# Order of the mLSTM gate rows, state loads and last normalisations around an RWKV-7 / mLSTM scan

## The chip, the cores and the metric

The kernel runs on one core of one Trainium2 chip. A core has five engines that run side by side, each through its own list of instructions: PE (matmul; its weight loads are shown apart as PEld), DVE (vector), ACT (scalar), POOL (GpSimd) and SP (here it only issues DMAs). An engine takes its instructions strictly in order, and an instruction that waits for a semaphore holds all behind it. DMAs are issued by SP, ACT or POOL, each into its own queue. The metric is the device time of one execution in microseconds; of the kernel before, three runs gave 2306.32, 2308.16 and 2311.97 us, so a median of 2308.16.

## The reference

One layer of a diffusion trunk, on 128 context tokens and 1024 latent tokens of width 1024. The context reads only itself; the latent tokens start each scan from a given state.

```python
h = rmsnorm(x, norm_g[0]) * (1 + sc1) + sh1           # sc1, sh1, g1 ... from silu(cond) @ ada_w
z_r, z_m, z_g = split(h @ w_in)                       # RWKV, mLSTM, branch gates
y_r, S = rwkv7_bidir(centred_shift(z_r), S0, ...)     # 8 heads x 64, both directions
y_m, (C, n, m) = mlstm_bidir(z_m, C0, n0, m0, ...)    # 4 heads x 128, both directions
merged = sigmoid(gr) * (y_r @ w_branch_rwkv) + sigmoid(gm) * (y_m @ w_branch_mlstm)
x = x + g1 * rmsnorm(merged @ w_out)
... gated ConvFFN: up, depthwise conv, silu, product, down
```

RWKV-7 updates a 64x64 state for each head, token and direction: `S = S*w - (S@kk) (kk*a)^T + v k^T`, `y = S@r`. The two directions are added, and each head is normalised over its 64 values (mean and variance), scaled, increased by a bonus term and multiplied by a gate `sigmoid(gd) @ g_up`. The mLSTM keeps a 128x128 state `C`, a vector `n` and a running maximum `m` for each head and direction. Its weights are exponentials of sums of gate logarithms less that maximum; its output, both directions added, is normalised over 128 values and gated by `sigmoid(o)`. The final states of the context are outputs.

## The kernel before

Tokens lie in nine blocks of 128, block 0 the context. Four parts follow one another, with overlap.

**Projection and preparation** (up to about 640 us): the combined projection in two-term products (`whi` and `wlo` times `act`, results in `pg`, copied out as `zraw` by ACT), the operands of both scans, and the triangular systems of all RWKV chunks (`La`, `Lb`, lines 522 and 524, on DVE and POOL).

**RWKV scan**: 18 steps over chunks of 64 tokens, both directions at once. `ORDER` gives the two chunks of a step: two context steps, then sixteen latent ones. `back` of step n begins with the matmuls `pP` (the state times the chunk's keys), which ACT copies to `Pm` (line 891). It goes on through `pU`, `pN` (the new state, `sn`) and `pY` (the outputs, copied or added into `ysum`). Between these stand, by `between(n)`, the `front` matmuls of step n+1 (`psc`, `pbk`, `pmh`, `pmt`, `pmb`; their results are copied by ACT as `A`, `BT`, `HT`, `TT` and masked by DVE as `KA`, `AB`), and groups of 24 projection matmuls by `fill` (the matmuls `pg` of the branch gates). `suv` holds a step's states and values; its values are loaded on POOL's queue (line 791), `XN` too (832); `KA`, `BKs` and the `TT` pieces are loaded on SP. Step 1's result is the context's final state; the latent steps start from `st`, loaded between (steps 1 and 2).

`rpost(b)` normalises a finished block b: a first half (mean, sum of squares, scaling of `ysum`) and a second half (transposes `pgt`, then scale, bonus `bon`, gate `pgg`, and the store `yrd`). `POST` tells after which step a block is begun: `{1: 0, 11: 4, 12: 5, 13: 3, 14: 6, 15: 2, 16: 7}`; blocks 1 and 8 follow after the last step. The two halves are apart by most of a step.

**mLSTM**: nine chunks of 128 for each direction, in 18 calls of `mback`, `mfront` one or two ahead. Its gate rows (`gates()`, six pieces) turn the gate logarithms of all tokens into tables, through sums, a running maximum along the chunks (`mm`, `mpv`) and a round trip through memory that turns it from rows into columns (`mpd` out, `mc` in, lines 1037 to 1044). `mback` ends with the outputs `hsum`, `mfinish` normalises a chunk.

**Merge, output projection, ConvFFN**: from about 1200 us; `y2r` and `y2m` are made from `yrd` and `ymd`, which come back from memory.

**What sets the order.** A scheduler lays out each engine's list by times that it simulates, from the program order and the dependences; so what has no late operand moves up. Instructions marked `keep_in_program_order` stay among each other as written. Before, this holds only for PE's, by an `Ordered` wrapper that is switched on from the scan to the end of the mLSTM. The gate pieces are written after steps 3 to 8, yet their rows are free to move. Tiles of a pool with one name, or tag, share memory: the next tile waits until the last one is read.

Of the kernel before, what the change touches and what calls it, by code (L numbers as in the profile page):

```python
# [57 lines left out]
def _body(tc, ctx, A, O, dbg, stop):  # L58
    nc = tc.nc
    v, s, gp = nc.vector, nc.scalar, nc.gpsimd  # L60
    dma = nc.sync.dma_start
# [13 lines left out]

    class Ordered:

        on = False

        def matmul(self, *a, **k):  # L80
            return self.keep(nc.tensor.matmul(*a, **k))  # L81

        def transpose(self, *a, **k):
            return self.keep(nc.tensor.transpose(*a, **k))
# [843 lines left out]
    def finish_ctx(sn):  # L928
        for d in range(2):
            pt = pss([128, 4, 64], "pfs")  # L930
            for p, h, hr in HP:
                pe.matmul(pt[hr, p, :], sn[hr, d, p, :], ident[hr, hr], start=True, stop=True)
            so = cp.tile([128, 4, 64], F32, name="so", tag="sn2", bufs=1)
            v.tensor_copy(so, pt)
            dma(O["s_rwkv"][0, 0, d].rearrange("(p h) i j -> (h i) p j", h=2), so)
# [657 lines left out]
```

## Time and profile before

| what | value |
|---|---|
| median of three runs | 2308.16 us (2306.32 to 2311.97) |
| the profiled execution | 2310.34 us, its span 2308.6 us |
| mean granted PE clock | 0.959 |
| PE busy | 2109.4 us, 91% |
| DVE busy | 1361.5 us, 59% |
| ACT busy | 847.8 us, 37% |
| POOL busy | 572.8 us, 25% |
| first `pP` of the scan | 650.49 us |
| last `pP` of the scan | 966.52 us |
| first latent `pmN` of the mLSTM | 1057.91 us |

All positions are microseconds from the span's start. A row of the timeline gives start, duration, engine, line, operation, `out<-in` and, in brackets, how long the engine stood idle before it and what released it. A row of a window gives its length, the busy time of PE, PEld, DVE, ACT and POOL with their instruction counts, the granted PE clock, the busy share of the DMA engines and GB/s. A row of a tile gives min/median/max in nanoseconds and the first and last start. A row of a group gives its count, then busy time and mean nanoseconds, then the idle time before, with what ended it. An engine's name with a q is its sequencer, which issues DMAs. Ordered calls carry the line of the wrapper (L81, L84), not of their own.

### The profile page before, as it was taken

The numbers are of one execution on the slowest core, as the hardware profiler recorded it, in microseconds if no ns is written. First come the engines' busy times: TensorE is split into PE (matmuls) and PEld (weight loads), VectorE is DVE, ScalarE is ACT, GpSimd is POOL, SyncE is SP. The second block draws the span as 40 slices with busy tenths as digits, with TensorE's granted clock in tenths as the row PEclk, the third lists the DMA queues.
The fourth block names the chain that finished last, engine by engine and source line by source line (L and its number), as shares of the span: only waits on it lengthen the run. The fifth ranks groups of instructions, "written<-read, shape, count | busy, mean of one in ns | idle before, by whom it ended". The sixth has DMA issues, their size and how long they took to land. (4 is left out here: it accounts for less than half of the span.)

```text
span 2308.6 us, 39893 instructions
## 1 busy us (share of the span) xinstructions
PE 2109.4 (91%) x16323; PEld 1944.2 (84%) x16323; DVE 1361.5 (59%) x2140; ACT 847.8 (37%) x1746; POOL 572.8 (25%) x725
## 2 busy tenths in 40 slices
PE   6999998988868998868869999999999999999996
PEld 4998998977857887868768978999999999999995
DVE  3666779789344556423544365646565656565558
ACT  3663646462233444445532143432212222222213
POOL 2000289888422233234612212000000000000004
PEclk9999998999978998979979999999999999999999
DMA  9144444445654554456657642202111111111104
GB/s 259 52 102 113 126 125 115 129 118 135 166 97 120 140 148 112 114 152 199 207 186 221 199 151 96 64 29 64 56 46 45 48 55 46 46 46 55 41 24 164
DMA packets 391413, 254.55 MB, mean 110 GB/s; under 512 B 86305, under 2 KB 368069, under 8 KB 391232
## 3 DMA queue, kind: packets, MB, share of 16 engines
q1 hardware_dynamic: 246864, 144.88, 22.6%
q10 hardware_dynamic: 135840, 88.03, 13.1%
q0 software_dynamic: 8528, 19.10, 3.3%
q8 instruction: 128, 2.10, 0.4%
q14 instruction: 53, 0.43, 0.1%
HBM read 186.73 MB, written 65.23 MB: 109 GB/s over the span
## 5 line engine op out<-in xcount | busy, mean ns | idle before, releaser
L81 PE MATMUL pg<-act,whi 128*128 128x384 f32 (+1 forms) x4416 | 856.0, 341 | 8.6 <-ACT zraw L537 5.6
L81 PEld LDWEIGHTS pg<-act,whi 128*128 128x128 f32 (+1 forms) x4416 | 778.1, 190 | 24.4 <-ACT zraw L537 6.0
L81 PE MATMUL pg<-act,wlo 128*128 128x384 f32 (+1 forms) x2208 | 436.1, 337 | 7.7 <-DVE wlo L364 7.7
L81 PEld LDWEIGHTS pg<-act,wlo 128*128 128x128 f32 (+1 forms) x2208 | 388.0, 188 | 11.2 <-DVE wlo L364 8.0
L364 DVE TENSOR_TENSOR wlo<-wraw,whi 128x1024 fp32r<-128x1024 f32 x130 | 163.5, 1259 | 217.8 <-ACT whi L363 217.6
L47 DVE SCALAR_TENSOR_TENSOR ua<-uraw,par,ua 128x945 f32<-128x945 f32 (+2 forms) x176 | 214.7, 1220 | 41.4 <-ACT ua L1485 38.2
L81 PE MATMUL pfd<-whi,f 128*128 128x512 f32 x792 | 227.5, 395 | 6.5 <-DVE facc L1557 6.5
L1559 POOL TENSOR_TENSOR x<-facc,grow 128x512 f32<-128x512 f32 x17 | 24.3, 1454 | 822.7 <-DVE facc L1557 822.7
L363 ACT ACTIVATE whi<-wraw 128x1024 fp32r<-128x1024 f32 x130 | 136.6, 1053 | 162.9 <-PE pg L81 103.3
L81 PEld LDWEIGHTS pfd<-whi,f 128*128 128x128 f32 x792 | 146.4, 188 | 37.2 <-DVE facc L1557 9.1
L1557 DVE TENSOR_TENSOR facc<-pfd,facc 128x512 f32<-128x512 f32 x180 | 122.1, 687 | 52.2 <-PE pfd L81 52.2
L524 POOL TENSOR_TENSOR Lb<-Lb,tmp 96x31 f32<-96x31 f32 (+15 forms) x155 | 130.3, 841 | 12.1
L522 POOL TENSOR_TENSOR tmp<-La,Lb 96x31 f32<-96x31 f32 (+15 forms) x155 | 121.2, 782 | 27.5 <-DMA La<-Ad 15.7
L81 PE MATMUL pfd<-wlo,f 128*128 128x512 f32 x396 | 122.6, 391 | 0.0
L1489 ACT ACTIVATE ua<-ua 128x1152 f32<-128x1152 f32 x22 | 25.7, 1168 | 219.4 <-DVE ua L47 219.4
L1499 ACT ACTIVATE f<-ua 128x384 fp32r<-128x384 f32 x66 | 32.1, 518 | 194.1 <-DVE ua L1498 194.1
L851 DVE TENSOR_TENSOR KA<-psc,msk 64x512 f32<-64x512 f32 x72 | 49.2, 684 | 84.2 <-ACT A L850 83.8
L81 PE MATMUL pwo<-whi,act 128*128 128x512 f32 x288 | 90.2, 393 | 1.1 <-ACT whi L363 1.1
L47 DVE SCALAR_TENSOR_TENSOR qacc<-zraw,par,qacc 128x945 f32<-128x945 f32 (+2 forms) x64 | 84.2, 1315 | 9.2 <-ACT qacc L580 8.7
L81 PEld LDWEIGHTS pfd<-wlo,f 128*128 128x128 f32 x396 | 74.3, 188 | 16.8
L791 POOL DMA_DIRECT2D suv<-Vd x72 | 42.5, 600 | 134.6 <-DVE sn L909 73.9
L1498 DVE TENSOR_TENSOR ua<-pg,ua 128x384 f32<-128x384 f32 x66 | 34.5, 553 | 68.9 <-PE pg L81 53.4
(368 smaller groups left out, 3085.0 us busy)
## 6 DMA issues: line engine op xcount, KB each, us to landing
wraw<-in_w_in ACTq DMA_DIRECT2D x44, 512.0 KB
wraw<-in_ffn_up ACTq DMA_DIRECT2D x44, 512.0 KB
zraw<-in_ada_w SPq DMA_DIRECT2D x24, 512.0 KB
wraw<-in_ffn_down ACTq DMA_DIRECT2D x22, 512.0 KB
KRd<-KR SPq DMA_DIRECT2D x24, 384.0 KB
sgz<-zraw ACTq DMA_DIRECT2D x16, 576.0 KB
KA<-KRd SPq DMA_DIRECT2D x72, 128.0 KB
BKs<-BKd SPq DMA_DIRECT2D x36, 256.0 KB
```

The costliest lines, as they stand in the source:

```text
L47: v.scalar_tensor_tensor(o, img[:, r0 + i:r1 + i, c0 + j:c1 + j], wt, o, op0=ALU.mult, op1=ALU.add)
L81: return self.keep(nc.tensor.matmul(*a, **k))
L363: s.activation(hi, raw, AF.Copy)
L364: v.tensor_tensor(lo, raw, hi.bitcast(F32), op=ALU.subtract)
L522: e.tensor_tensor(t3, L[:, j, i].unsqueeze(2).to_broadcast([NI, n, m]), X[:, j:j + 1, c].to_broadcast([NI, n, m]), op=ALU.mult)
L524: e.tensor_tensor(X[:, i, c], X[:, i, c], t3, op=ALU.subtract)
L791: pdma(suv[r, d, h].rearrange("t x p n -> t x (p n)"), src.unsqueeze(1).to_broadcast([64, 2, 4 * LC]))
L851: v.tensor_tensor(q.KA[orr, :, h, :], sc_[h][orr], msk[orr, d:d + 1, :].to_broadcast([64, 4, 128]), op=ALU.mult)
L1489: s.activation(ua, ua, AF.Silu)
L1498: v.tensor_tensor(ua[:, gs], pt, ua[:, gs], op=ALU.mult)
L1499: s.activation(f2[:, 0, gs], ua[:, gs], AF.Copy)
L1557: v.tensor_tensor(acc[:, b, qs], pt, acc[:, b, qs], op=ALU.add)
```

## The change

1. `Ordered` wraps any engine. `pinned(it)` keeps the rows of DVE, ACT, POOL and SP in program order during one piece of `gates()`, so that the six pieces stand after steps 3 to 8 where they are written.
2. `state_load()` loads both RWKV states ahead of the loads of step 0, `init_state` transposes them before step 1's `back`, and `finish_ctx` is put into a list `due`, from which `between` takes one entry in each step.
3. `rpost`: `ysum` is centred by one DVE addition, squared by one ACT row and summed by one DVE reduction, in place of eight ACT squares with accumulation; and scaled by one DVE multiplication in place of eight. The load of `bon` and the store `yrd` go from SP's queue to POOL's, and `bon` is loaded in the second half. That half now follows the middle of `merge` in the next step.
4. Blocks 1 and 8 are normalised within the mLSTM's context chunk. The scan's pools are closed earlier, `rpost`'s pool later; the context's `hsum` has a tile of its own, `h0`. The mLSTM states are loaded before the context chunk and transposed within it.
5. `mback` adds a direction's outputs into `hsum` with four DVE rows that read PSUM, in place of a DVE product and a POOL addition. `vx` has two buffers in place of three. Two groups of 24 `pg` matmuls move from before the latent chunks and from the last `mfinish` loop to the fill behind the mLSTM.

```diff
+    def pinned(it):
+
+        for e in (v, s, gp, sy):
+            e.on = True
+        next(it)
+        for e in (v, s, gp, sy):
+            e.on = False
...
-    rpc = ExitStack()
-    rp = pool("rpost", 1, rpc)
-    ysp = pool("ysp", 1, rpc)
+    rp = pool("rpost", 1, mpc)
+    cpc = ExitStack()
+    ysp = pool("ysp", 1, cpc)
...
+    def state_load():
+
+        st = rp.tile([128, 2, 4, 64], F32, name="st0", tag="yt")
+        for d in range(2):
+            dma(st[:, d], A["state_rwkv"][0, 0, d].rearrange("(p h) i j -> (h i) p j", h=2))
+        return st
...
-            st = cp.tile([128, 4, 64], F32, name="st0", tag="sn2", bufs=1)
-            dma(st, A["state_rwkv"][0, 0, d].rearrange("(p h) i j -> (h i) p j", h=2))
-            pt = pss([128, 4, 64], "pst")
             for p, h, hr in HP:
-                pe.matmul(pt[hr, p, :], st[hr, p, :], ident[hr, hr], start=True, stop=True)
+                pe.matmul(pt[hr, d, p, :], st[hr, d, p, :], ident[hr, hr], start=True, stop=True)
...
-        bon = rp.tile([128, 4, 128], F32, name="bon", tag="bon")
-        dma(bon, bond[:, :, bs].rearrange("p c t -> c p t"))
...
+        v.tensor_tensor(y, y, mu.unsqueeze(2).to_broadcast([128, 8, 64]), op=ALU.add)
+        sq = rp.tile([128, 8, 64], F32, name="sqy", tag="bon")
+        s.activation(sq, y, AF.Square)
         va = rp.tile([128, 8], F32, name="yva", tag="yva", bufs=2)
-        for i in range(8):
-            s.activation(sq, y[:, i], AF.Square, bias=mu[:, i:i + 1], accum_out=va[:, i:i + 1])
+        v.tensor_reduce(va, sq, axis=mybir.AxisListType.X, op=ALU.add)
         v.tensor_scalar(va, va, 1.0 / 64, 64e-5, op0=ALU.mult, op1=ALU.add)
         gp.tensor_tensor(va, va, mhalf, op=ALU.pow)
-        for i in range(8):
-            v.tensor_scalar(y[:, i], y[:, i], mu[:, i:i + 1], va[:, i:i + 1], op0=ALU.add, op1=ALU.mult)
+        v.tensor_tensor(y, y, va.unsqueeze(2).to_broadcast([128, 8, 64]), op=ALU.mult)
         yield
+        bon = rp.tile([128, 4, 128], F32, name="bon", tag="bon")
+        pdma(bon, bond[:, :, bs].rearrange("p c t -> c p t"))
...
-        dma(yrd[:, :, bs].rearrange("p c t -> c p t"), yt)
+        pdma(yrd[:, :, bs].rearrange("p c t -> c p t"), yt)
...
             scores(n + 1, d, qs[d])
-            if d == 1 and posts:
-                next(posts.pop())
             yield
         m = merge(qs)
         next(m)
+        if due:
+            due.pop(0)()
         fill(2)
...
         if n == 1:
-            finish_ctx(sn)
-            nxt = new_suv(n + 1)
-            init_state(True, nxt)
-        suv = nxt
+            due.append(lambda sn=sn: finish_ctx(sn))
+        if n in POST:
+            r = rpost(POST[n])
+            next(r)
+            due.append(lambda r=r: next(r))
         if 2 < n < 9:
-            next(gate)
-        if n in POST:
-            posts.append(rpost(POST[n]))
-            next(posts[-1])
-    for b in (1, 8):
-        r = rpost(b)
-        next(r)
-        fill(2)
-        next(r)
-    rpc.close()
+            pinned(gate)
+    cpc.close()
...
-            ht = mp.tile([128, 2, 2, 128], F32, name="ht", tag="ht", bufs=1)
-            v.tensor_tensor(ht, pn[:, :, :, 0:128], den.unsqueeze(3).to_broadcast([128, 2, 2, 128]), op=ALU.mult)
-            gp.tensor_tensor(hs, hs, ht, op=ALU.add)
+            for h in range(4):
+                o = hs[:, h // 2, h % 2, :]
+                v.scalar_tensor_tensor(o, pn[:, h // 2, h % 2, 0:128], den[:, h // 2, h % 2:h % 2 + 1], o,
+                                       op0=ALU.mult, op1=ALU.add)
...
     qs = [mload(*dc) for dc in SEQ[0:3]]
+    sts = [state_loads(d) for d in range(2)]
+    rps = [rpost(b) for b in (1, 8)]
+    next(rps[0])
     for q in qs[0:2]:
         mfront(q)
+    next(rps[1])
+    fill(2)
...
         CNs[d] = mback(qs[i], CNs[d])
+        if i < 2:
+            next(rps[i])
+            sts[d] = state(d, *sts[d])
...
         if i == 1:
-            states_out(CNs)
-            CNs = state(True)
-            fill(2)
+            for e in range(2):
+                state_out(e, CNs[e])
+            CNs = sts
...
     for m in fins:
         next(m)
-        fill(4)
+        fill(2)
```

Three places show what the scheduler makes of it. ACT during the preparation, before (`zraw`: copies of the projection; `gf`, `bb`, `dc`: gate rows; `A`, `BT`: the first scan steps' operands):

```order
L537 ACTIVATE zraw<-pg 128x384 x2
L1055 ACTIVATE gf<-GG,mcs 128x128
L363 ACTIVATE whi<-wraw 128x1024
L1049 ACTIVATE bb<-bb 128x128
L1058 ACTIVATE dc<-dc 128x1
L537 ACTIVATE zraw<-pg 128x384
L355 DMA wraw<-in_w_in 128x8x128
L539 DMA sgz<-zraw 128x1152
L850 ACTIVATE A_5815<-psc_5800 32x128
L850 ACTIVATE A_5815<-psc_5801 32x128
L856 ACTIVATE BT<-pbk 128x512
```

The same rows now, on ACT between the scan's steps 6 and 7:

```order
L889 ACTIVATE TT_5726<-pmt 32x4x32 x2
L69 ACTIVATE bb<-bb 128x128
L69 ACTIVATE gf<-GG,mcs 128x128
L69 ACTIVATE dc<-dc 128x1
L900 ACTIVATE Pm<-pP 128x512
L859 ACTIVATE A_8029<-psc_8014 32x128
L859 ACTIVATE A_8029<-psc_8015 32x128
L865 ACTIVATE BT<-pbk 128x512
```

They moved from before the first step's `A` to before the seventh step's `Pm`. On DVE the gate rows now stand at the same place:

```order
L920 TENSOR_TENSOR suv<-sn,WL 64x2x256 x2
...
L69 COPY mpv_7693<-mm_7692 4x7
L69 TENSOR_TENSOR mx<-mc,bG 128x1
L69 TENSOR_SCALAR GG<-GG,mc 128x128
L69 TENSOR_TENSOR bb<-bb,GG 128x128
L69 TENSOR_SCALAR mcs<-mc 128x1
L69 TENSOR_TENSOR dc<-mc,mx 128x1
L860 TENSOR_TENSOR KA<-psc_7753,msk 64x4x128
L862 TENSOR_TENSOR AB_5728<-psc_7753,msk 64x4x64
```

Between the update of the states (`suv<-sn`) and the next step's `KA`, eight rows of the running maximum and five that use `mc` have come in. PE at the end of the scan, before (`pgt`, `pgg`: second halves of blocks 1 and 8; `pmP`: first of the mLSTM):

```order
L81 MATMUL pY<-suv,AB_5731 64x64
L81 MATMUL pg<-act_160,whi 128x384 x16
L81 MATMUL pg<-act_160,wlo 128x384 x8
L81 MATMUL pg<-act_161,whi 128x384 x16
L81 MATMUL pg<-act_161,wlo 128x384 x8
L81 MATMUL pgt<-ident,ysum 64x64 x16
L81 MATMUL pgg<-sgd_10686,gup 128x128 x4
L81 MATMUL pg<-act_159,whi 128x384 x16
L81 MATMUL pg<-act_159,wlo 128x384 x8
L81 MATMUL pgt<-ident,ysum 64x64 x16
L81 MATMUL pgg<-sgd_10770,gup 128x128 x4
L81 MATMUL pmP<-qk 128x128 x4
```

and now:

```order
L69 MATMUL pY<-suv,AB_5731 64x64
L69 MATMUL pg<-act_160,whi 128x384 x16
L69 MATMUL pg<-act_160,wlo 128x384 x8
L69 MATMUL pmP<-qk 128x128 x4
L69 MATMUL pmk<-ident,qk 128x128 x8
L69 MATMUL pg<-act_161,whi 128x384 x16
L69 MATMUL pg<-act_161,wlo 128x384 x8
...
L69 MATMUL pmC<-vx,kw 128x129 x4
L69 MATMUL pgt<-ident,ysum 64x64 x16
L69 MATMUL pgg<-sgd_10652,gup 128x128 x4
L69 MATMUL pmi<-ident,cn_10644 128x128 x4
L69 MATMUL pmi_10821<-ident,nr_10646 128x4
L69 MATMUL pmP<-qk 128x128 x4
```

The mLSTM's first `pmP` moved ahead of both normalisations, whose transposes now follow the context chunk's state product `pmC`. On POOL, the rows of block 1's second half (`yt`, `yrd`) now stand among the mLSTM's masks (`MI`):

```order
L1197 TENSOR_TENSOR MI<-MI,mbig 128x512
L980 TENSOR_TENSOR yt<-yt,bon 128x512
L969 DMA bon<-bond 128x4x128
L985 DMA yrd<-yt 128x4x128
L1213 TENSOR_TENSOR MI<-qk,MI 128x512
L1195 MEMSET vx 128x4
L1197 TENSOR_TENSOR MI<-MI,mbig 128x512
```

Before, `yt` of both blocks stood ahead of the first `MI`, and the two DMAs on SP.

More of the change, by code (lines that the diff above doesn't have):

```diff
@@ L776, in _body @@
                 gp.memset(ABs[d][i][64 - 64 * h:128 - 64 * h, :, h, :], 0.0)
-    cp = pool("scan", 2, rpc)
+    cp = pool("scan", 2, cpc)
     seen = set()
@@ L793, in new_suv, with init_state @@
         return suv
-    def init_state(latent, suv):
-        if not latent:
+    def state_load():
[3 more added lines that the diff above has]
+        return st
+    def init_state(st, suv):
+        if st is None:
             for h in range(2):
@@ L928, in finish_ctx @@
     def finish_ctx(sn):
+        pt = pss([128, 2, 4, 64], "pfs")
         for d in range(2):
-            pt = pss([128, 4, 64], "pfs")
             for p, h, hr in HP:
[L932 to L935, printed above, removed]
+                pe.matmul(pt[hr, d, p, :], sn[hr, d, p, :], ident[hr, hr], start=True, stop=True)
+        so = rp.tile([128, 2, 4, 64], F32, name="so", tag="yt")
+        v.tensor_copy(so, pt)
+        for d in range(2):
+            dma(O["s_rwkv"][0, 0, d].rearrange("(p h) i j -> (h i) p j", h=2), so[:, d])
     gup = rp.tile([128, 512], F32, name="gup", bufs=1)
@@ L1148, in _body, with hs_of @@
     banks(pg=2, ps=2, pf=2)
-    hsum = yhp.tile([128, NB, 4, 128], F32, name="hsum", tag="yh")
+    h0 = mp.tile([128, 4, 128], F32, name="h0", tag="h0", bufs=1)
+    hsum = []
     seen, Ss = set(), {}
+    def hs_of(c):
+        if c == 0:
+            return h0
+        if not hsum:
+            hsum.append(yhp.tile([128, NB - 1, 4, 128], F32, name="hsum", tag="yh"))
+        return hsum[0][:, c - 1]
     def pair(name):
@@ L1234, in mfinish @@
     def mfinish(c):
-        h3 = hsum[:, c]
+        h3 = hs_of(c)
         mu = mf.tile([128, 4], F32, name="mu", tag="mu")
@@ L1257, in mfinish @@
         yield
-    def state(latent):
-        CNs = []
-        for d in range(2):
-            CN = mp.tile([128, 4, 130], F32, name="CN", tag=f"CN{d}")
-            if not latent:
-                gp.memset(CN, 0.0)
-            else:
-                cn = mf.tile([128, 4, 128], F32, name="cn0", tag="sqm")
-                dma(cn, A["state_mlstm_C"][0, 0, d].rearrange("h v k -> v h k"))
-                nr = mf.tile([4, 128], F32, name="nr0", tag="nr0")
-                dma(nr, A["state_mlstm_n"][0, 0, d])
-                pt = psf([128, 4, 128], "pmi")
-                for h in range(4):
-                    pe.transpose(pt[:, h, :], cn[:, h, :], ident)
-                v.tensor_copy(CN[:, :, 0:128], pt)
-                pt = psf([128, 4], "pmi2")
-                pe.transpose(pt, nr, ident[0:4, 0:4])
-                v.tensor_copy(CN[:, :, 128], pt)
-            CNs.append(CN)
-        return CNs
@@ new lines, in state_loads, with state_out @@
+    def state_loads(d):
+        cn = mf.tile([128, 4, 128], F32, name="cn0", tag="sqm")
+        dma(cn, A["state_mlstm_C"][0, 0, d].rearrange("h v k -> v h k"))
+        nr = mf.tile([4, 128], F32, name="nr0", tag="nr0")
+        dma(nr, A["state_mlstm_n"][0, 0, d])
+        return cn, nr
+    def state_out(d, CN):
+        pt = psf([128, 4, 128], "pmo")
+        for h in range(4):
+            pe.transpose(pt[:, h, :], CN[:, h, 0:128], ident)
+        co = mf.tile([128, 4, 128], F32, name="co", tag="sqm")
+        v.tensor_copy(co, pt)
+        dma(O["s_C"][0, 0, d].rearrange("h v k -> v h k"), co)
+        pt = psf([4, 128], "pmo2")
+        pe.transpose(pt, CN[:, :, 128], ident)
+        no = mf.tile([4, 128], F32, name="no", tag="nr0")
+        v.tensor_copy(no, pt)
+        dma(O["s_n"][0, 0, d], no)
```

83 lines of the change are left out of this document (41 added, 42 removed).

## The prediction

> **What bounds the kernel now.** The chain that ended last stops after one row here, so I read the windows (busy time of each engine in a stretch), then the timeline of PE between the marks of the program, then the groups of rows that a wait named.
>
> ```profile
> core 0: us, PE busy (x) PEld busy (x) DVE busy (x) ACT busy (x) POOL busy (x), PEclk, DMA share, GB/s
> 628.00:702.00 74.00, 42.82 (x757) 38.19 (x757) 28.28 (x64) 20.09 (x62) 12.92 (x21) 0.72 0.48 98
> 967.00:1060.00 93.00, 67.31 (x567) 63.26 (x564) 28.26 (x64) 35.15 (x114) 31.03 (x33) 0.80 0.48 143
> 1230.00:2309.00 1079.00, 1052.54 (x5853) 967.50 (x5845) 632.22 (x879) 290.57 (x495) 71.11 (x54) 0.99 0.24 76
> ```
>
> After 1230 PE is busy for 1052.54 of 1079 us, and the change leaves its order alone there: nothing is to be had. In 628 to 702 it is busy for 42.82 of 74 us, and the granted clock is 0.72: PE waits, and then works slowly. 967 to 1060 is like it. PE's order is fixed by the program through the scan and the mLSTM, so one late operand holds all that follows. A step of the scan begins with the matmuls `pP`; the distance between two such marks is a step.
>
> **Head, 575 to 650 us.** The scheduler hoisted the gate rows of the mLSTM (`gf`, `bb`, `mc`) to where PE projects and the triangular solves run.
>
> ```profile
> 594.72 0.29 DVE L993 SCALAR_TENSOR_TENSOR bb<-gf 128x128 f32<-128x128 f32 x1 [9.64 <-DMA gf<-gtd]
> 595.04 0.31 ACT L994 ACTIVATE bb<-bb 128x128 f32<-128x128 f32 x1 [14.62 <-DVE bb L993]
> 596.73 5.36 PE L81 MATMUL pg<-act,whi 128*128 128x384 f32 x16 [5.65 <-ACT zraw L537]
> 597.09 1.28 ACT L995 ACT_TABLE_LOAD   x1 [0.41 <-ACT zraw L537]
> 603.32 2.93 PE L81 MATMUL pg<-act,whi 128*128 128x384 f32 x16
> 628.37 1.16 PE L81 MATMUL psc<-KA,BKs 64*128 64x128 f32 x16
> 635.61 0.24 SPq L1037 DMA_DIRECT2D mpd<-mpv  x1
> 639.42 0.16 DVE L1044 TENSOR_TENSOR mx<-mc,bG 128x1 f32<-128x1 f32 x1 [2.88 <-DMA mc<-mpd]
> 639.87 0.40 ACT L1055 ACTIVATE gf<-GG,mcs 128x128 f32<-128x128 f32 x1 [12.67 <-DVE mcs L1053]
> 644.03 2.67 PE L81 MATMUL psc<-KA,BKs 64*128 64x128 f32 x16 [13.91 <-ACT BT L856]
> 650.49 1.98 PE L81 MATMUL pP<-suv,KA 128*64 128x64 f32 x32
> 908.29 0.49 PE L81 MATMUL psc<-KA,BKs 64*128 64x128 f32 x2 [1.55 <-ACT BT L856]
> ```
>
> ACT stood 14.62 us before `bb` and 12.67 us before `gf`. Queued behind them on ACT are the copies of PE's results (`zraw`, then `A` and `BT` of the first scan step); behind the 9.64 us on DVE stand rows of the solve. PE pays 5.65 and 13.91 us, and its work afterwards is slower: 5.36 us for sixteen `pg` against 2.93, 2.67 for sixteen `psc` against 1.16. With the gate rows gone, 13.91 falls to a wait of the ordinary kind (1.55, the row of 908.29). Gain: 5.65 + 2.43 + 13.91 + 1.51 - 1.55 = **21.9 us**. If the solve, freed of the 9.64, still ends as late, only the first two terms come: 8 is the low end, and 24, without the ordinary wait, the high one.
>
> **Steps 0 to 3.**
>
> ```profile
> 654.69 2.20 PE L81 MATMUL psc<-KA,BKs 64*128 64x128 f32 x16 [2.22 <-DMA BKs<-BKd]
> 696.94 1.12 PE L81 MATMUL pst<-ident,st 64*64 64x64 f32 x16 [11.35 <-DMA st<-in_state_rwkv]
> 700.40 1.12 PE L81 MATMUL pst<-ident,st 64*64 64x64 f32 x16 [2.34 <-DMA st<-in_state_rwkv]
> 701.45 2.15 PE L81 MATMUL pP<-suv,KA 128*64 128x64 f32 x32
> 722.59 1.15 PE L81 MATMUL pP<-suv,KA 128*64 128x64 f32 x32
> 737.59 1.15 PE L81 MATMUL pP<-suv,KA 128*64 128x64 f32 x32
> 752.19 1.15 PE L81 MATMUL pP<-suv,KA 128*64 128x64 f32 x32
> ```
>
> Steps 3 and 4 are the undisturbed ones: 722.59 to 737.59 to 752.19, so 15.00 and 14.60 us. Steps 0 and 1 together run from 650.49 to 701.45, 50.96 us. In step 0 PE waits 2.22 us for `BKs`, issued on SP behind the gates' transfers, and works slowly; in step 1 the two state loads are issued only once their buffer `sn2` is free, and PE waits 11.35 and 2.34. Loaded before step 0 and transposed ahead of the step, the states leave 15.0 and 14.60 + 1.15 (the 32 small matmuls, at `pP`'s price for 32): 30.75, **20.2 gained**; at least the three waits, 15.9. Step 2 takes 21.14: the context's final state and the late start of block 0's second half. It keeps the final-state transposes (15.75, gain 5.4), and block 0's second half goes to step 3, which grows by its 32 small matmuls, 1.15, and four wider ones, some 0.75: net **3.5**, and 0 if step 3 waits as step 2 did.
>
> **Gate rows within steps 3 to 8.** The same six pieces now stand between the scan's rows on DVE, ACT, POOL and SP, pinned. Three pay visibly: three table loads of 1.28 us on ACT in steps 4 and 5, ahead of `Pm`, for which PE waits at once; and after step 6 DVE's `mx`, which waits for `mpd` to go out and `mc` to come back. That took 639.42 - 635.61 = 3.8 us. Queued behind `mx` are DVE's `KA` of the next step, and behind `dc` on ACT the `Pm`. So 3.84 + 3.8 = 7.6, and some 4 us for clock and late operands behind two such holds (the head lost 3.9 us of clock to two): **12 us lost**. Below it lies 0, if fills and earlier loads cover all (not less: the steps only get rows added); above, what the three waits of ACT and DVE cost in the head, 9.64 + 12.67 + 14.62 = 37. I stay near the low end because the loads of a step are issued a step early, so SP has about 15 us of slack.
> The Trainium skill, "ScalarE: Activation LUTs", What ACT_TABLE_LOAD costs, adds a drain of about 1.38 us to each load of 1.28. In the trace `bb` follows such a load within 0.01 us, and 0.41 us was idle before it. By the page three loads would cost an estimated 4.1 us more; I go by the row.
>
> **Normalisation and steps 12 to 16.**
>
> ```profile
> 859.10 1.15 PE L81 MATMUL pP<-suv,KA 128*64 128x64 f32 x32
> 925.00:943.00 18.00, 16.84 (x368) 15.46 (x368) 11.47 (x21) 7.66 (x23) 4.66 (x7) 1.00 0.83 203
> 966.52 1.15 PE L81 MATMUL pP<-suv,KA 128*64 128x64 f32 x32
> ...
> L954 ACT ACTIVATE sqy<-ysum,ymu x72: 331/348/356, 683.1 to 1001.7; 128x64 f32<-128x64 f32 x72
> L954 ACT ACTIVATION_READ_ACCUMULATOR sqy<-ysum,ymu x72: 185/187/208, 683.4 to 1001.9; 128x1 f32 x72
> L949 DVE TENSOR_REDUCE ymu<-ysum x9: 675/686/689, 682.2 to 984.9; 128x8 f32<-128x512 f32 x9
> L891 ACT ACTIVATE Pm<-pP x18: 597/597/602, 654.0 to 967.8; 128x512 f32<-128x512 f32 x18
> L958 DVE TENSOR_SCALAR ysum<-ysum,ymu,yva x72: 303/310/1337, 690.3 to 1005.6; 128x64 f32<-128x64 f32 x72
> ```
>
> A block cost ACT 8 x (0.348 + 0.187) = 4.28 us in one piece; it now costs one `Square` of 128x512, by the row of `Pm` 0.60. DVE loses eight rows of 0.31 (2.48) and gains an add, a reduction and a multiplication of 128x512, 3 x 0.69 = 2.06. The second half is now taken up later in the step, so that PE meets its `pgt` when `ysum` is ready. Steps 12 to 16 last 966.52 - 859.10 = 107.42 us. The one least disturbed fills the window 925 to 943: 16.84 us of PE work at clock 1.00. With 0.7 us of waits, 5 x 17.5 = 87.5: **19.9**. At most it is 23 (no waits); at least 11.5, if only the path to `pgt` gets shorter, by 4.28 - 0.60 - 2 x 0.69 = 2.3 in each of the five. Step 17, which now holds a second half, **loses 1**.
>
> **`bon` and `yrd` on POOL's queue.** No `bon` or `yrd` issue of POOL is in the trace; the nearest are
>
> ```profile
> L791 POOL DMA_DIRECT2D suv<-Vd x72 | 42.5, 600 | 134.6 <-DVE sn L909 73.9 <-PE pmh L81 28.5 <-ACT HT L867 25.2
> ```
>
> They took 0.60 us each; `yrd` and `bon` come in four times as many pieces, so 0.60 to 2.4, and two of them 1.2 to 4.8 a block. POOL stood idle for 134.6 us ahead of those issues, 7.5 us for each of the 18 steps: that covers it, and I take 0. If the cover is gone, seven blocks cost 8 to 34. On SP two transfers go; nothing there was awaited.
> The Trainium skill, "SBUF — State Buffer", SBUF: two separate sides, warns of this move: descriptors of POOL's queue are written by GpSimd, and wait while DVE holds the shared port; it gives 3100 ns for a transfer that alone takes 620. The 72 `suv` issues, amid DVE work, average 600 ns, so the trace shows nothing of it. By the page two transfers for each of seven blocks would add an estimated 14 x 2.5 = 35 us on POOL.
>
> **Last blocks within the context chunk.**
>
> ```profile
> 982.39 3.07 PE L81 MATMUL pg<-act,whi 128*128 128x384 f32 x16
> 1004.54 1.76 PE L81 MATMUL pgt<-ident,ysum 64*64 64x64 f32 x28 [3.76 <-DVE ysum L958]
> 1016.58 2.05 PE L81 MATMUL pmP<-qk 128*128 128x128 f32 x8 [8.25 <-issue]
> 1027.05 0.77 PE L81 MATMUL pmN<-vx,MI 128*128 128x129 f32 x2 [4.49 <-DMA vx<-vmd]
> 1048.72 1.09 PE L84 MATMUL pmi<-ident,cn 128*128 128x128 f32 x4 [4.55 <-DMA cn<-in_state_mlstm_C]
> 1057.91 0.38 PE L81 MATMUL pmN<-vx,MI 128*128 128x129 f32 x2
> ```
>
> From the scan's end to the first latent `pmN` 75.52 us pass. Two `pg` groups of 24 leave this stretch for the end of the mLSTM (8.8 us at 2.93 for 16, no gain). The waits shown are 3.76 + 8.25 + 4.49 + 4.55 = 21.05, and rows slower than others of their form, at a clock of 0.80, cost about 6 by my count: 27 at most. Loads of `qk`, `vx` and states now go earlier, but block 1's `yt` stands on POOL behind the mask addition of a later chunk, which needs a buffer that the context's `pmN` frees. I take a little over six tenths: **16.6**. At the other end is a loss as long as the 8.25, if that hold becomes a wait of its own.
>
> **mLSTM and branch merge.**
>
> ```profile
> 1137.37 1.15 PE L84 MATMUL pmf<-ident,hsum 128*128 128x128 f32 x4 [3.30 <-DVE hsum L1246]
> 1201.07 0.69 PE L81 MATMUL pbr<-y2r,whi 128*128 128x384 f32 x1 [10.85 <-ACT y2r L1344]
> ```
>
> Direct accumulation on DVE takes POOL's add out of the path to `pmf` and adds about 0.4 us of DVE a chunk: **3** (0 to 3.3). `pbr` waits 10.85 us for `y2r`; `yrd` is complete earlier and three more `pg` groups precede it, yet `y2m` still has its own trip: **4** (0 to 10.85).
>
> **Sum.** -21.9 - 20.2 - 3.5 + 12 - 19.9 + 1 - 16.6 - 3 - 4 = -76.1. From the profiled execution's 2310.3 us: 2234.2. That execution is 2.2 us above the median of the runs, 2308.2, so **2232 us** on their scale.
>
> **Rivals.** *Gates as dear as before*: the pinned pieces hold DVE and ACT for the full 37 us, since every step's rows queue behind them; for it speaks the pinning, which lets nothing past; against it that PE's fills lie between. 2232 + 25 = 2257. *The transition gains nothing*: `yt` behind the mask holds POOL and with it the masks of the latent chunks: 2232 + 16.6 = 2249. *Slower, POOL as the bound*: `bon` and `yrd` hold POOL beyond the 7.5 us of idle time, so that `suv` comes late in each of steps 3 and 12 to 17. It decides once POOL loses over 7.5 + 76/7 = 18.4 us a block, 9 us for each issue against 0.60 shown: 2315 or more. The rule of the Trainium skill's page on SBUF points that way; its 2.5 us an issue would stay within the 7.5. *It does not do what it says*, a new wait eating all: 2308; for it speaks only that DVE and ACT stay in one order with PE, against it that the waits named are taken away row by row.
>
> **Chances.** Forecast 0.62; gates dear 0.17; transition empty 0.16; POOL bound 0.03; no change 0.02. About 0.3%, 7 us, is what this kernel's measurement tells from nothing. Faster 0.95, same 0.02, slower 0.03. The range: below, gates free (-12), the transition's whole 27 (-10) and a further 10 from the clock, 2200; above, the dearer of the two middle rivals with half of the other's loss and POOL's, 2257 + 13 = 2270.
>
> **What would show it.** `pP` of step 0 near 629 us and no PE wait over 5 us before it; steps 0 to 2 at 15 to 16 us; steps 4 to 7 some 2 to 4 us longer than 14.6, with ACT or DVE waits on `mc` and `bb`; steps 12 to 16 near 17.5; first latent `pmN` some 50 us after the scan. It is wrong if steps 3 to 8 together grow by over 25 us, if `suv` releases PE's waits, or if the solve keeps `pP` past 640.

## The result, and the profile after

The changed kernel takes 2248.8 us (median of four runs, 2246.24 to 2252.67), against 2309.2 of the kernel before (four runs, 2306.32 to 2311.97): a ratio of 0.974, 95% interval 0.9721 to 0.9759, so some 60 us less. The forecast was 2232. The profiled executions span 2308.6 and 2244.5 us, 64.1 apart; the sum of the prediction, 76.1, is to be held against those.

| stretch (from mark to mark) | before | after | difference | forecast |
|---|---|---|---|---|
| start to first `pP` | 650.49 | 634.36 | -16.1 | -21.9 |
| steps 0 and 1 | 50.96 | 32.06 | -18.9 | -20.2 |
| steps 2 and 3 | 36.14 | 33.12 | -3.0 | -3.5 |
| steps 4 to 9 (gate rows) | 92.09 | 106.43 | +14.3 | +12 |
| steps 10 and 11 | 29.42 | 29.17 | -0.3 | 0 |
| steps 12 to 16 | 107.42 | 87.82 | -19.6 | -19.9 |
| last `pP` to first latent `pmN` | 91.39 | 74.23 | -17.2, of it 8.8 moved on | -15.6, and 8.8 moved on |
| latent mLSTM to first `pwo` | 284.37 | 280.94 | -3.4, with 8.8 moved in | -7, with 8.8 moved in |
| the rest | 966.3 | 966.4 | 0 | 0 |

With the 8.8 us of moved `pg` groups set right (120 `pg` matmuls in the transition against 168), the transition gave 8.4 us where 15.6 stood in the sum, and the mLSTM with the merge 12.2 where 7 did.

The windows of the kernel after, cut at the marks of the scan: first its length, then the busy time of PE, PEld, DVE, ACT and POOL, the granted PE clock, the DMA share and GB/s. The first row is steps 0 to 3, the second 4 to 9, the fourth 12 to 16, the last the transition.

```profile
core 0: us, PE busy (x) PEld busy (x) DVE busy (x) ACT busy (x) POOL busy (x), PEclk, DMA share, GB/s
634.40:699.50 65.10, 63.80 (x1258) 58.06 (x1256) 38.66 (x65) 25.60 (x68) 23.51 (x40) 0.96 0.55 140
699.50:806.00 106.50, 93.35 (x1741) 83.60 (x1734) 54.50 (x109) 42.29 (x108) 27.27 (x51) 0.94 0.51 124
...
835.10:923.00 87.90, 83.16 (x1650) 75.47 (x1642) 64.59 (x112) 38.89 (x98) 40.23 (x51) 1.00 0.56 142
923.00:997.20 74.20, 55.08 (x512) 51.59 (x510) 32.31 (x49) 26.90 (x75) 32.80 (x36) 0.86 0.56 168
```

Of the kernel before, steps 12 to 16 and 4 to 9:

```profile
859.10:966.50 107.40, 90.52 (x1646) 82.03 (x1640) 63.42 (x144) 53.88 (x186) 32.98 (x41) 0.89 0.47 119
737.60:829.70 92.10, 88.22 (x1737) 79.86 (x1733) 49.67 (x84) 37.52 (x100) 24.99 (x44) 0.98 0.57 141
```

Steps 0 to 3 are now nearly all PE work, and steps 12 to 16 run at clock 1.00 instead of 0.89. In steps 4 to 9 PE's work takes 93.35 us where it took 88.22, at a clock of 0.94 instead of 0.98: 5.1 of the 14.3 us lost there are the same matmuls run slower. What is left to gain stands in the second and the last row.

The timeline of the kernel after, PE's waits and what was in their way:

```profile
624.36 1.06 ACT L367 ACTIVATE whi<-wraw 128x1024 fp32r<-128x1024 f32 x1 [2.62 <-DMA wraw<-in_w_in]
627.89 2.67 PE L850 MATMUL psc<-KA,BKs 64*128 64x128 f32 x16 [6.40 <-ACT BT L865]
634.36 1.98 PE L69 MATMUL pP<-suv,KA 128*64 128x64 f32 x32
715.84 1.28 ACT L69 ACT_TABLE_LOAD   x1
718.08 1.28 ACT L69 ACT_TABLE_LOAD   x1
733.01 1.28 ACT L749 ACT_TABLE_LOAD   x1
787.84 1.11 ACT L889 ACTIVATE TT<-pmt 32x128 f32<-32x128 f32 x4 [5.83 <-DMA TT<-Xtd]
789.34 0.47 PE L69 MATMUL pgt<-ident,gi 128*128 128x128 f32 x1 [6.99 <-ACT gi L69]
948.85 0.66 PE L69 MATMUL pmk<-ident,qk 128*128 128x128 f32 x4 [2.99 <-ACT S L1205]
958.49 0.77 PE L69 MATMUL pmN<-vx,MI 128*128 128x129 f32 x2 [4.79 <-DMA vx<-vmd]
971.95 0.26 PE L69 MATMUL pmi<-ident,nr 4*128 4x4 f32 x1 [4.49 <-DVE yt L984]
988.85 1.43 PE L69 MATMUL pmP<-qk 128*128 128x128 f32 x5 [3.09 <-DVE yt L984]
```

The 13.91 us before the second group of `psc` became 6.40, not 1.55: the gate rows are gone, but ACT, before it copies the operands, is held by its own DMA issues and by a weight load that they start late (more of this under `decb` late). The three table loads took the 1.28 us each that was forecast, all in step 5. The 6.99 us in step 8 were named by no part of the prediction. In the context chunk four waits remain, 15.4 us together.

### The profile page after: what moved, and what is told of

It reads as the page before. It is cut to its first block, busy times and chain, and to the rows that moved or that the text cites. A ratio compares the mean times of both kernels' runs of the same rounds, so it can differ in the third digit from the quotient of the medians.

```text
span 2244.5 us, 39723 instructions
## 1 busy us (share of the span) xinstructions
PE 2092.5 (93%) x16323; PEld 1929.4 (86%) x16323; DVE 1376.8 (61%) x2119; ACT 823.5 (37%) x1611; POOL 578.9 (26%) x734
## 3 DMA queue, kind: packets, MB, share of 16 engines
q1 hardware_dynamic: 237360, 140.16, 22.3%
## 5 line engine op out<-in xcount | busy, mean ns | idle before, releaser
L381 PE MATMUL pg<-act,whi 128*128 128x384 f32 (+1 forms) x3808 | 723.0, 337 | 0.5 <-DVE act L344 0.4
L381 PEld LDWEIGHTS pg<-act,whi 128*128 128x128 f32 (+1 forms) x3808 | 664.2, 188 | 12.7 <-DVE act L344 0.7
L381 PE MATMUL pg<-act,wlo 128*128 128x384 f32 (+1 forms) x1904 | 373.8, 336 | 4.5 <-DVE wlo L368 4.5
L381 PEld LDWEIGHTS pg<-act,wlo 128*128 128x128 f32 (+1 forms) x1904 | 333.4, 187 | 7.9 <-DVE wlo L368 4.8
L69 PE MATMUL pg<-act,whi 128*128 128x384 f32 x496 | 99.3, 349 | 0.0
L381 PEld LDWEIGHTS pfd<-wlo,f 128*128 128x128 f32 x396 | 74.3, 188 | 16.8
L69 PEld LDWEIGHTS pg<-act,whi 128*128 128x128 f32 x496 | 87.2, 193 | 0.6
```

The costliest lines, as they stand in the source:

```text
L69: return (lambda *a, **k: tc.keep_in_program_order(f(*a, **k))) if self.on else f
L381: pe.matmul(out, wt(hw, k), at(ha, k), start=(i == 0), stop=(i == last))
```

## The experiments

All are the changed kernel with one edit, unless said otherwise; each ratio is to the kernel before, in runs on the same chip. The changed kernel's is 0.974 (0.9721 to 0.9759); 0.001 is 2.3 us. Differences of 11 us and more between a run and the changed kernel are those of the two ratios.

### The gate rows free again

```diff
-            pinned(gate)
+            next(gate)
```

> The changed kernel, except that the six gate pieces are no longer pinned, so the scheduler may hoist their rows again. Theory: pinning moved a cost more than it removed one. The two traces show the first pP 16.1 us earlier, and steps 4 to 9 together 14.2 us longer (106.4 against 92.2). Without pinning the first pP should go back to 646 to 652 us, steps 4 to 9 to 92 to 95 us, and the time stay within 6 us of the changed kernel's 2249. Rival: the gain at the head is real and the longer steps have another cause; then the time rises by 14 to 18 us, to about 2265, with steps 4 to 9 still above 103 us.

2252.0 us, ratio 0.9757 (0.9739 to 0.9775). The first `pP` comes at 647.72 us, steps 4 to 9 take 91.6: 13.4 us lost at the head and 14.8 won back in the scan. On PE in the preparation:

```profile
596.18 4.21 PE L381 MATMUL pg<-act,whi 128*128 128x384 f32 x12 [6.94 <-ACT zraw L541]
641.24 2.67 PE L850 MATMUL psc<-KA,BKs 64*128 64x128 f32 x16 [11.87 <-ACT BT L865]
```

So the first theory holds: where the gate rows stand decides where they are paid, hardly how much. Pinning is worth nothing that these runs can tell (the intervals overlap); the 60 us come from the other parts.

### The states loaded late

```diff
-    st0 = state_load()
...
-        if n == 1:
-            init_state(st0, nxt)
...
+        if n == 1:
+            finish_ctx(sn)
+            nxt = new_suv(n + 1)
+            init_state(True, nxt)
```

(with the loads and the tiles of the kernel before in `init_state` and `finish_ctx`)

> The changed kernel, but the RWKV states are loaded, and the context's final state written, between steps 1 and 2 as before. Theory: PE again waits 11 and 2 us for the two loads, and the late start of block 0's second half does not come back; steps 1 to 3 together rise from 47.7 us to 64 to 68, the time by 16 to 20 us, to 2265 to 2269. Rival: with the gate rows gone from SP's queue the loads come sooner, the wait is mostly hidden, and the time rises by no more than 6 us.

2265.7 us, ratio 0.9809 (0.9788 to 0.9829), 16 us above the changed kernel. Steps 1 to 3 take 64.6 us. PE's waits are those of the kernel before (11.35 and 2.34 there), though no gate row stands on SP by then:

```profile
674.68 1.12 PE L69 MATMUL pst<-ident,st 64*64 64x64 f32 x16 [10.53 <-DMA st<-in_state_rwkv]
678.29 1.12 PE L69 MATMUL pst<-ident,st 64*64 64x64 f32 x16 [2.49 <-DMA st<-in_state_rwkv]
```

The rival is out. SP issues the loads from 672.32 on, behind the stores of `so` (from 666.80), which shares their buffer `sn2`, as the prediction had it. The run puts back the late place in the program and the shared buffer together, and does not part the two.

### Narrow normalisation, and the second half early

Two edits in two runs. The first puts back the eight squares and eight scalings; the second takes what is due between the scores.

```diff
-        v.tensor_tensor(y, y, mu.unsqueeze(2).to_broadcast([128, 8, 64]), op=ALU.add)
-        sq = rp.tile([128, 8, 64], F32, name="sqy", tag="bon")
-        s.activation(sq, y, AF.Square)
+        sq = rp.tile([128, 64], F32, name="sqy", tag="bon")
...
-        v.tensor_reduce(va, sq, axis=mybir.AxisListType.X, op=ALU.add)
+        for i in range(8):
+            s.activation(sq, y[:, i], AF.Square, bias=mu[:, i:i + 1], accum_out=va[:, i:i + 1])
...
+        for i in range(8):
+            v.tensor_scalar(y[:, i], y[:, i], mu[:, i:i + 1], va[:, i:i + 1], op0=ALU.add, op1=ALU.mult)
```

> The changed kernel, but the first half of rpost computes as before: eight ACT squares with accumulation and eight DVE scalings for each block. Theory (the shares of the prediction): the path to pgt grows by 2.3 us a block and ACT is held 3.7 us longer, so steps 12 to 16 rise from 87.8 us by about 11, the time by 10 to 16 us. Rival: the gain in steps 12 to 16 came from the later place of the second half; then the narrow rows are covered, and the time stays within 4 us of 2249.

```diff
             scores(n + 1, d, qs[d])
+            if d == 1 and due:
+                due.pop(0)()
             yield
         m = merge(qs)
         next(m)
-        if due:
-            due.pop(0)()
```

> The changed kernel, but what is due (second halves, the context's final state) is taken between the scores of the next step, as before, ahead of the middle of merge. Theory: the wide rows alone make ysum ready in time, so steps 12 to 16 rise from 87.8 us by at most 4, and the time by 0 to 5 us. Rival: the later place carries the gain; then pgt waits again by 2 to 4.5 us in each of five steps, and the time rises by 10 to 20 us.

Narrow rows: 2277.4 us, ratio 0.9867 (0.9842 to 0.9891), 29 us above the changed kernel. Early second half: 2264.0 us, ratio 0.9807 (0.979 to 0.9823), 15 us above. Steps 12 to 16 take 107.5 us with the narrow rows and 103.0 with the early half, against 87.8 with both edits in place and 107.4 before. So neither alone keeps more than 4.4 us of the 19.6: the parts do not add up, and my division of the gain between them, 11.5 at least for the rows, has no ground. The windows of these steps, of the run with narrow rows and of the run with the early half:

```profile
840.70:948.24 107.54, 90.98 (x1646) 82.62 (x1640) 60.69 (x135) 51.85 (x181) 39.38 (x50) 0.90 0.45 116
```

```profile
834.54:937.52 102.98, 90.51 (x1646) 82.44 (x1640) 61.91 (x113) 38.41 (x98) 41.74 (x52) 0.90 0.48 125
```

PE's waits in the timeline, with narrow rows:

```profile
868.37 1.86 PE L69 MATMUL psc<-KA,BKs 64*128 64x128 f32 x13 [3.84 <-DVE AB L862]
890.50 1.18 PE L69 MATMUL psc<-KA,BKs 64*128 64x128 f32 x14 [2.85 <-DVE AB L862]
913.80 1.12 PE L69 MATMUL pbk<-ident,BKs 128*128 128x128 f32 x4 [3.42 <-DVE AB L862]
934.42 1.16 PE L69 MATMUL psc<-KA,BKs 64*128 64x128 f32 x14 [2.82 <-DVE AB L862]
```

and with the early second half:

```profile
864.41 1.63 PE L69 MATMUL pgt<-ident,ysum 64*64 64x64 f32 x32 [2.16 <-DVE AB L862]
885.40 1.97 PE L69 MATMUL pgt<-ident,ysum 64*64 64x64 f32 x32 [2.19 <-DVE AB L862]
```

With narrow rows PE waits not for `ysum` but for `AB`, the next step's operand. Ahead of the first of these waits stand, on DVE and ACT:

```profile
862.32 0.17 DVE L963 TENSOR_SCALAR yva<-yva 128x8 f32<-128x8 f32 x1 [4.31 <-ACT sqy L962]
862.81 0.54 ACT L859 ACTIVATE A<-psc 32x128 f32<-32x128 f32 x2
865.30 1.87 DVE L966 TENSOR_SCALAR ysum<-ysum,ymu,yva 128x64 f32<-128x64 f32 x8 [2.81 <-POOL yva L964]
867.19 0.69 DVE L860 TENSOR_TENSOR KA<-psc,msk 64x512 f32<-64x512 f32 x1
```

The copy `A`, for which `KA` waits in other steps, is done at 863.35, but in DVE's list `KA` and `AB` stand behind the block's own rows: DVE waits for ACT's squares (ACT is busy for 51.85 us in these steps against 38.89), then for POOL's `yva`, scales `ysum`, and only then takes `KA`. The other three waits look the same. With the early half `ysum` is ready, as the theory had it (its scaling ends at 857.05 in the first of the two cases), but `pgt`, due at 862, waits for `AB`, which it does not read: `pgt` takes one of the three PSUM banks of the ring `pf`, and `psc` holds that bank until `AB` has read it. Each such wait is short, but PE's clock in the stretch is 0.90 instead of 1.00, and the 83.2 us of PE work become 91: more than a third of the loss is work that runs slower. Without this share the narrow rows lose 11.9 us, 2.4 a step, about the 2.3 by which the prediction took the path to be longer. Block 0's first half costs the same way: step 2 takes 23.0 us with narrow rows, 16.5 without.

### `bon` and `yrd` on SP's queue

```diff
-        pdma(bon, bond[:, :, bs].rearrange("p c t -> c p t"))
+        dma(bon, bond[:, :, bs].rearrange("p c t -> c p t"))
...
-        pdma(yrd[:, :, bs].rearrange("p c t -> c p t"), yt)
+        dma(yrd[:, :, bs].rearrange("p c t -> c p t"), yt)
```

> The changed kernel, but bon is loaded and yrd stored through SP's queue, as before. Theory (the prediction): POOL's idle time covers the two issues and SP has room, so the time stays within 4 us of the changed kernel's 2249. Rival: on POOL they hold suv and XN, so that taking them away gives 6 us or more. Second rival: on SP the store's wait for yt holds the loads behind it, and the time rises by 6 us or more.

2245.4 us, ratio 0.9734 (0.9718 to 0.9751): no difference that can be told, and neither rival's 6 us. Within the profiled execution the transition is 5.0 us shorter, and the part from there to the first `pwo` 6.7 longer; 6.0 of these are PE work that runs slower (255.5 us busy against 249.5, at a clock of 0.94 against 0.97). Why the clock was lower there, the traces do not show.

### SP in program order

```diff
             pinned(gate)
+            sy.on = n < 8
```

> The changed kernel, but SP's rows stay in program order from the first gate piece to the last, so that decb, which waits until dcd has landed, stands behind the loads of TT and KA of the next steps and not among them. Theory: the 5.83 us for which ACT waits for TT in step 8, and the 6.99 us of PE behind it, come from that wait in SP's queue; step 8 falls from 23.3 us to 15 to 17, and the time by 5 to 9 us, to 2240 to 2244. Rival: TT is late for want of DMA bandwidth or of its buffer; then step 8 stays above 21 us and the time within 3 us of 2249.

2279.1 us, ratio 0.9882 (0.9865 to 0.9898), 33 us above the changed kernel: neither theory nor rival. Step 8 is 33.2 us long, step 5 29.2. The waits in SP's own queue and the two longest of PE:

```profile
SPq L69 <- DVE bG L69: 19.7, 2, 18.6
SPq L69 <- ACT dc L69: 13.9, 1, 13.9
```

```profile
736.18 1.19 PE L69 MATMUL psc<-KA,BKs 64*128 64x128 f32 x6 [13.35 <-DMA BKs<-BKd]
801.59 1.83 PE L69 MATMUL psc<-KA,BKs 64*128 64x128 f32 x13 [13.94 <-DMA BKs<-BKd]
```

SP's stores of the gates wait up to 18.6 us for DVE and 13.9 for ACT, and in program order the loads of the next step wait with them. Steps 4 to 9 take 134.0 us, 42 more than before: a loss of the size of the rival "gates as dear as before" (37), though here the pieces hold SP's queue and not, as it had it, ACT and DVE. In the changed kernel it stays away because only the gate pieces are kept in order, and the scheduler puts the loads ahead of them.

### `decb` late, and `mx` late

```diff
+        yield
         dma(decb, dcd.rearrange("d r -> (d r)").unsqueeze(0).to_broadcast([128, 72]))
...
-        if 2 < n < 9:
+        if 2 < n < 10:
```

> The changed kernel, but the load of decb is a piece of its own, one step later, after step 9; SP's other rows are as free as in the changed kernel. Theory: in the changed kernel decb, waiting for dcd to land, stands among the TT loads and makes step 8 late. A step later dcd has landed, step 8 falls from 23.3 us to 15 to 17, and the time by 5 to 9 us. Rival: TT is late for want of DMA bandwidth; then step 8 stays above 21 us and the time within 3 us of the changed kernel's.

2249.9 us, ratio 0.9744 (0.9715 to 0.9774). Step 8 still takes 22.3 us, with a wait of 6.82 on PE, and the TT loads come as late, with `decb` behind them: the theory falls. In the second run the piece that begins with `mx` also follows a step later:

```diff
-        if 2 < n < 9:
+        if n in (3, 4, 5, 6, 8, 9, 10):
```

> As the run decb_late, and the piece that begins with mx comes after step 8, not 7, so that mc is in place when DVE reaches mx. Theory: DVE's 6.6 us before mx go, step 7 falls from 17.6 us to about 15 and the time by another 2 to 3 us, 8 to 12 below the changed kernel. Rival: step 7 is held by something else (its scatter over the runs so far is 15.4 to 20.0 us), and nothing more is gained than in decb_late.

2245.4 us, ratio 0.9723 (0.969 to 0.9756). Steps 7 and 8 take 14.6 and 14.5 us, but steps 9 and 10, where the pieces now are, 18.5 each: of steps 4 to 11, 135.6 us in the changed kernel, 131.1 are left. So step 8 was held by the pieces that now come later, the one with `mx` and the one behind it (`gi`, `pgt`), which moved along; steps 7 and 8 gain 11.8 us by it, and steps 9 and 10 lose 6.2. The traces point to the stores of the piece with `mx`, which wait on SP for ACT. In the run with `decb` late, SP's waits between 760 and 792 us:

```profile
SPq L69 <- ACT dc L69: 5.0, 1, 5.0
SPq L75 <- DMA dcd<-dc: 2.2, 1, 2.2
```

The way from SP to ACT is an odd one, and it is read off the trace and the program, as no run changed it alone. ACT's row of 787.84 copies `pmt`, and is released in the trace by a load, `TT<-Xtd`, that it does not read (both write into `TT`). Ahead of it ACT issues two DMAs of its own (`wraw`, `sgz`). In the built program the rows at this place, each with the semaphores that it waits for, are:

```
L749 ACTIVATE zraw<-pg 128x384 [waits PE_49]
L359 DMA wraw<-in_w_in 128x8x128 [waits DMAHW5_49]
L751 DMA sgz<-zraw 128x1152 [waits DMAHW6_49,Activation_49]
L889 ACTIVATE TT_5725<-pmt 32x4x32 [waits PE_49]
```

In the program DMAs of SP and ACT take the semaphores DMAHW0 to DMAHW7 in turn, and these issues wait for an earlier DMA that used their own; the count of DMAHW5 that `wraw` waits for is brought by a load `TT<-Xtd` of SP's. The copy waits for PE alone. So ACT's `wraw` stood behind a late load of SP's, and the copy, which did not need it, behind `wraw`. The head's 6.40 us look the same: ACT stood 10.05 us before a `zraw`, and the two issues ahead of it, of `wraw` and `sgz`, wait in the program for SP's loads `TT<-Xtd` and `KA<-KRd`. The hold was there in the kernel before, too, 9.83 us at the `zraw` that stands ahead of `gf`. The row of the kernel after, and that of the kernel before:

```profile
620.87 0.87 ACT L541 ACTIVATE zraw<-pg 128x384 f32<-128x384 f32 x2 [10.05 <-DMA KA<-KRd]
```

```profile
626.32 0.87 ACT L537 ACTIVATE zraw<-pg 128x384 f32<-128x384 f32 x2 [9.83 <-DMA TT<-Xtd]
```

### Two turns within the context chunk

```diff
     qs = [mload(*dc) for dc in SEQ[0:3]]
-    sts = [state_loads(d) for d in range(2)]
     rps = [rpost(b) for b in (1, 8)]
     next(rps[0])
     for q in qs[0:2]:
         mfront(q)
+    sts = [state_loads(d) for d in range(2)]
```

> The changed kernel, but the mLSTM state loads are written behind the two mfront of the context chunk, so that vx is issued ahead of them on SP. Theory: PE's 4.79 us for vx in the context chunk come from the four state loads ahead of it in the queue; the wait falls below 1.5 us and the time by 2 to 5 us, unless the states are then late. Rival: PE waits there for MI as well, which comes at the same time; then the time stays within 1.5 us of 2249.

```diff
         if i < 2:
-            next(rps[i])
             sts[d] = state(d, *sts[d])
+            next(rps[i])
```

> The changed kernel, but within the context chunk the mLSTM states are transposed ahead of the second halves of blocks 1 and 8. Theory: the waits of 4.49 and 3.09 us before pmi and pmP come from their PSUM banks, held by pgg until the last DVE row of the second half, which is late by POOL's queue; with the order turned they fall to under 4 us together, and the time by 2 to 5 us. Rival: the wait only moves on to the next user of those banks, and the time stays within 1.5 us of 2249.

`vx` first: 2248.0 us, ratio 0.9749 (0.9731 to 0.9767). The wait for `vx` did come from the loads ahead of it, since it falls from 4.79 to 0.86 us,

```profile
958.65 0.46 PE L69 MATMUL pmN<-vx,MI 128*128 128x129 f32 x2 [0.86 <-DMA vx<-vmd]
```

and the transition is 5.2 us shorter; but the part from there to the first `pwo` is 4.2 longer (3.8 of it PE work that runs slower, at a clock of 0.95 against 0.97), and the time does not show it. States first: 2251.4 us, ratio 0.9759 (0.9735 to 0.9782); the waits of 4.49 and 3.09 us turn into 4.46, 1.54 and 2.52 before `pmP` and `pgt`. There the rival holds: the wait moves to the next user of the banks.

### Blocks 1 and 8 ahead of the mLSTM

```diff
+    for b in (1, 8):
+        r = rpost(b)
+        next(r)
+        fill(2)
+        next(r)
     cpc.close()
...
-    rps = [rpost(b) for b in (1, 8)]
-    next(rps[0])
...
-    next(rps[1])
-    fill(2)
...
-            next(rps[i])
```

> The changed kernel, but blocks 1 and 8 are normalised after the scan and ahead of the mLSTM, as before; qk, vx and the mLSTM states are still loaded early. Theory (from the traces: the stretch from the last pP to the first latent pmN gave 8.3 us beyond the moved pg groups): the time rises by 6 to 12 us. Rival: interleaving them gained nothing, as PE now waits for yt within the chunk; then the time stays within 3 us of 2249.

2251.9 us, ratio 0.9752 (0.9719 to 0.9785): the rival, or no more than a few us. PE now waits 5.69 and 3.92 us for `ysum` ahead of the mLSTM,

```profile
955.40 1.97 PE L69 MATMUL pgt<-ident,ysum 64*64 64x64 f32 x32 [5.69 <-DVE ysum L966]
968.06 1.97 PE L69 MATMUL pgt<-ident,ysum 64*64 64x64 f32 x32 [3.92 <-DVE ysum L966]
```

no longer for `vx`, and only 1.66 us for a bank that `yt` holds. Interleaving exchanged one set of waits for another. What the transition gained is left, by elimination, to the loads of `qk`, `vx` and states that go ahead; no run put these back alone.

### The pieces that helped, together

The edits of `mx` late and of SP's queue for `bon` and `yrd`.

> As the run mx_late, and bon and yrd on SP's queue as in the run sp_queue. Theory: steps 12 to 16 and the mLSTM's context chunk do not depend on which of the two queues carries them, so the time is that of mx_late within 3 us: about 2238, the fastest so far. Rival: POOL was held by its two issues in the transition, and the time falls by a further 3 us or more.

2239.3 us (2235.28 to 2239.73), ratio 0.9692 (0.9665 to 0.972): the fastest of all, 11 us below the changed kernel, though its interval only just clears that one's. First `pP` at 633.83, steps 4 to 11 131.7 us, transition (by the state product `pmC`) 70.6 against 76.0, and this time the part up to the first `pwo` does not grow. The number is the theory's, but the run with `mx` late alone had come out at 2245, so these 6 us more are what the rival asked for. In both pairs of runs that differ by this queue alone, the transition (to the first latent `pmN`) is 5 us shorter with SP's: 69.3 against 74.2 us, and 68.8 against 74.0. That speaks for the rival; the intervals of the two times overlap, and it stays open.

## Why the prediction came out as it did

The sign and the places of the gains were right, and the three largest terms stayed the three largest; the sum was 12 us too large. The time happens to be that of the rival "the transition gains nothing", 2249, but by chance: the transition did gain 8.4 us, and the rest of the shortfall lies elsewhere. Two things that were to show it did not come: a wait over 5 us was left before the first `pP` (6.40), and the first latent `pmN` stands 57.8 us after the scan and not some 50. By its own steps:

- **Head**, 16.1 of 21.9. The step "13.91 falls to a wait of the ordinary kind (1.55)" failed: 6.40 remained, and 1.51 of slow clock behind it. Next in line was the hold of ACT's own DMA issues by loads of SP's; it stood in the old trace (9.83 us), but the prediction quoted the pieces of ACT's queue ahead of `BT` only as victims of the gate rows.
- **Steps 0 to 3**, 21.9 of 23.7. Right, and by the run with the states loaded late for the reason given, a buffer that is free late, together with the later place of the loads in the program.
- **Gate rows in the scan**, 14.3 against 12. The size was right, in part by luck, as half of the make-up was wrong. Step 5 with its table loads lost 4.5 us and step 7, where DVE waits 6.6 us for `mc`, 2.4. The clock took 5.1, near the 4 counted for clock and late operands. But step 8 lost 6.2, in a place where I had given SP "about 15 us of slack". The mean also hides scatter: over the runs that leave these pieces alone, steps 4 to 9 take 105 to 111 us.
- **Steps 12 to 16**, 19.6 of 19.9. The number rested on a step of the old trace that was already undisturbed, and held. The explanation beside it did in part: the wide rows do shorten the path through squares, `yva` and `ysum`, by about the 2.3 us a step that it counted, but what waited at its end was not `pgt`: it was the next step's `KA` and `AB`, behind it in DVE's list. And the rows pay only with the later second half: alone they kept 4.4 us, where the prediction had at least 11.5.
- **Transition**, 8.4 of 15.6. I counted six tenths of the waits as gone. The hold that I named, `yt` behind a mask on POOL, was there (4.49 and 3.09 us), and `vx`, which I took to go earlier, was issued behind the four state loads.
- **mLSTM and merge**, 12.2 of 7. The waits of `pmf` stayed, 7.8 us after against 7.7 before: POOL's addition no longer stands in the path, but DVE's scaling ahead of `pmf` still waits for POOL's `va`. That term, 3, was nothing. `y2r` still holds PE, only now at a `pg` ahead of `pbr`, whose copy stands behind `y2r` on ACT: 7.05 us against 10.85. Of the 12.2 us, 7.2 came between the first `pbr` and the first `pwo`, 5.0 of these PE work that runs faster (clock 0.99 against 0.93). No step of the prediction names that; that this surplus makes up for part of what the head and the transition fell short is luck. The rows after:

```profile
1131.91 2.46 ACT L1367 ACTIVATE y2r<-zraw 128x1152 fp32r<-128x1152 f32 x2 [10.06 <-DMA zraw<-yrd]
1136.69 5.33 PE L746 MATMUL pg<-act,whi 128*128 128x384 f32 x16 [7.05 <-ACT zraw L749]
```

- **POOL's queue**, nothing forecast, and nothing that the times can tell. `bon` and `yrd` were issued in 0.80 and 0.77 us, within the bounds given; what the queue costs in the transition stays open. By the figures of the Trainium skill's page "SBUF — State Buffer" (section "SBUF: two separate sides"), 3100 ns against 620, a transfer from this queue would by estimate take some 2.5 us longer beside a DVE `tensor_copy`; no run here shows that.

Of the 16.8 us between forecast and median, 12.0 are these terms. The rest is scatter: the profiled execution of the kernel before stood 2.2 us above the median that I scaled by, that of the changed kernel 2.6 below its own.

## What to carry to other kernels

The gate rows, with their round trip through memory, cost about the same in both places of this full schedule (13.4 us at the head, 14.8 in the scan): ask first which queue such work holds there (here SP for its stores, ACT for its tables, DVE for its load), and spread its pieces before moving the whole. A gain that rests on two edits should be measured with each undone: here each alone kept 0 and 4.4 of 19.6 us. When a wait names a row that the waiting one does not read, look for what stands between them, in the list or in a shared buffer. And where an engine issues DMAs, look among its waits for loads that it does not read.
